# Four Strassen quads in each output projection of a two-layer decoder trunk, and six raw weight buffers

## The chip, the cores and the metric

The kernel runs on one core of a Trainium2 chip. Its time is the device time of one execution in microseconds, as the median of several; it was 2072.09 us over three runs (2071.94 to 2075.0). A core has five engines, each with its own queue of instructions: TensorE (PE in the profile: matmuls, with the weight loads as PEld), VectorE (DVE), ScalarE (ACT), GpSimd (POOL) and SyncE (SP), which here only issues transfers. Transfers run on 16 DMA engines.

## The reference

A decoder trunk of two layers over 256 tokens of width 2048, float32. Each layer is attention and then a gated feed-forward network with a causal convolution of width 3, each followed by a residual and a layer norm:

```python
for layer in range(DEPTH):                      # 2
    if layer < N_A_LAYERS:
        attn = moba_attention(h, moba_w_qkv[layer], moba_w_o[layer], rel_bias)
    else:
        attn = swa_attention(h, swa_w_q[j], swa_sinks[j], swa_w_o[j], k_band, v_band, ...)
    h = layer_norm(ALPHA * h + attn, ln_g[layer, 0], ln_b[layer, 0])
    ffn = conv_ffn(h, ffn_w_up[layer], ffn_conv_w[layer], ffn_conv_b[layer], ffn_w_down[layer])
    h = layer_norm(ALPHA * h + ffn, ln_g[layer, 1], ln_b[layer, 1])
```

The output projection at the end of an attention is `o @ w_o`, a 256 x 2048 by 2048 x 2048 product; the down-projection at the end of a feed-forward network is 256 x 5504 by 5504 x 2048.

## The kernel before, in words

**Precision.** Every float32 operand is split in a high and a low part (`float32r`), and a product is three matmuls: high by high, high by low, low by high (`product`, L503 to L511).

**Weights.** They come as a stream of halves: 128 x 1024 float32, 512 KB, which is two blocks of 128 x 512. `load_weights` (L135) loads a half into one of `RAW_BUFS` = 5 raw buffers from SP's queue. `high_upto` (L149) copies it to its high part on ScalarE (L159), `low_piece` (L166) subtracts on VectorE for the low part (L168). Both go to one of `HALF_BUFS` = 4 pairs of buffers, and TensorE reads them there. `split_upto(i)` splits up to half i and, after each, issues the load that takes the raw buffer that has become free. `take()` (L203), called before a half is used, splits up to three halves ahead (`AHEAD`). Where `reach` names a half, it splits further ahead, into memory that is idle by then (`aside`, `home`): the last eight halves of a projection (`WINDOW`) are run for token tile 0 first and then for token tile 1, so that all eight have to be there at once, and the layer norm of tile 0 runs beside tile 1's matmuls.

**Order.** The order is written out by hand. Work besides the matmuls is put on an agenda: `at(n, f)` queues f for VectorE, ScalarE and the queues n slots later, `pe_at` for TensorE. A slot is one half (`step`). Within `take()` the splits come first and then the slot's agenda; in a half that `reach` names, the agenda runs before the splits as well.

**Strassen quads.** In the down-projections, for two blocks of rows (a pair) and two chunks of 512 columns, the four weight blocks B11, B12, B21, B22 against two token tiles would be eight products. Seven are made, with sums of weights T1 to T4 and sums of activations. `presums` (L417) makes the weight sums during earlier stages: two loads of 512 KB on SP's queue, three subtractions or additions on VectorE (L427, L430, L431), and a store of 1 MB to DRAM on GpSimd's queue; the sums then come back as two halves of the stream, (T1, T3) and (T2, T4). `sums(i)` (L560) makes the activation sums of a group of two pairs in three steps on the agenda: `whole` adds high and low part (L566), `combine` makes the sums in a second work buffer (L575), `split` makes their high part on ScalarE (L579) and their low part on VectorE (L580), in memory of `xT`, which is idle then. A group of two pairs is seven halves (`SEVEN`); `PLAINS` says how many plain halves stand ahead of each group. `fold` (L536) adds the four products P1, P5, P6, P7 of two chunks to the result. A plain half has twelve matmuls, a half of a quad six.

**The output projections** (`project_out`, called at L826) have no quads before: 32 plain halves, chunk after chunk. The heads' outputs, which they read, are made by `attention`; the last heads' outputs come in the projection's first slots.

## Time and profile before

| | |
|---|---|
| Median of three runs | 2072.09 us |
| The profiled execution's own time | 2071.97 us |
| Its span, first to last instruction | 2070.2 us |
| TensorE busy | 2049.3 us (99%) |
| VectorE busy | 1656.4 us (80%) |
| ScalarE busy | 1039.4 us (50%) |
| DMA | 520.48 MB, 251 GB/s mean |
| Mean granted clock of TensorE | 0.998 |

The stages, by the busy time in each: layer 0's attention to 301 us, its output projection to 392, the opening of the feed-forward network to 444, the rest of its up-projection to 877, the down-projection to 1101; then layer 1 in the same order, with its output projection from 1260 to 1352 and its down-projection from 1837 on. A line of the timeline is: start, duration, engine, line, operation, out<-in, shapes, count, and in brackets how long the engine had stood idle before it and what ended that. Matmuls overlap, so a matmul's duration is longer than the distance to the next.

### The profile page before, as it was taken

The numbers are of one execution on the slowest core, as the hardware profiler recorded it, in microseconds if no ns is written. First come the engines' busy times: TensorE is split into PE (matmuls) and PEld (weight loads), VectorE is DVE, ScalarE is ACT, GpSimd is POOL, SyncE is SP. The second block draws the span as 40 slices with busy tenths as digits, with TensorE's granted clock in tenths as the row PEclk, the third lists the DMA queues.
The fourth block names the chain that finished last, engine by engine and source line by source line (L and its number), as shares of the span: only waits on it lengthen the run. The fifth ranks groups of instructions, "written<-read, shape, count | busy, mean of one in ns | idle before, by whom it ended". The sixth has DMA issues, their size and how long they took to land.

```text
span 2070.2 us, 29436 instructions
## 1 busy us (share of the span) xinstructions
PE 2049.3 (99%) x10956; PEld 1770.5 (86%) x10956; DVE 1656.4 (80%) x2388; ACT 1039.4 (50%) x1471; POOL 46.5 (2%) x76
## 2 busy tenths in 40 slices
PE   9999999999999999999999999999999999999997
PEld 7888888888888888888888888898888888888886
DVE  5666567689888888888786787679898888888877
ACT  4444445344444444465663455435444444456563
POOL 0100000000000000000000000000000000000000
PEclk9999999999999999999999999999999999999999
DMA  8757757368878778788884866737787877868894
GB/s 284 268 193 254 274 174 256 107 225 278 278 273 276 271 277 267 241 279 291 291 302 154 286 218 237 254 113 271 268 282 269 274 272 270 274 223 296 271 317 148
DMA packets 140190, 520.48 MB, mean 251 GB/s; under 512 B 18528, under 2 KB 18848, under 8 KB 133648
## 3 DMA queue, kind: packets, MB, share of 16 engines
q1 hardware_dynamic: 126992, 457.08, 65.4%
q0 software_dynamic: 12768, 61.27, 7.7%
q8 instruction: 86, 1.41, 0.3%
q14 instruction: 56, 0.46, 0.1%
q10 hardware_dynamic: 288, 0.26, 0.0%
HBM read 474.42 MB, written 48.28 MB: 252 GB/s over the span
## 4 chain that ended last, share of the span: by engine, by line
PE 93%; DVE 4%; DMA 1%; ACT 1%; issue 1%; SPq 0%; DVEq 0%; ACTq 0%
PE acc L313 37%; PE acc L315 19%; PE acc L509 7%; PE acc L510 7%; PE acc L511 7%; PE acc L376 2%; PE acc L377 2%; PE acc L378 2%; PE at L510 2%; PE at L511 2%; PE at L509 2%; PE acc L340 1%; DVE wl L168 1%; DMA raw<-in_wst_dram 1%; PE at L696 1%
## 5 line engine op out<-in xcount | busy, mean ns | idle before, releaser
L168 DVE TENSOR_TENSOR wl<-raw,wh 128x1024 fp32r<-128x1024 f32 (+1 forms) x723 | 863.1, 1220 | 158.2 <-ACT wh L159 142.3
L159 ACT ACTIVATE wh<-raw 128x1024 fp32r<-128x1024 f32 (+1 forms) x723 | 740.0, 1054 | 238.7 <-PE acc L511 92.8
L313 PE MATMUL acc<-xT,wh 128*128 128x512 f32 x3456 | 832.7, 392 | 0.0
L313 PEld LDWEIGHTS acc<-xT,wh 128*128 128x128 f32 x3456 | 641.2, 188 | 128.4
L315 PEld LDWEIGHTS acc<-xT,wl 128*128 128x128 f32 x3456 | 444.1, 190 | 17.1 <-DVE wl L168 4.4
L315 PE MATMUL acc<-xT,wl 128*128 128x256 f32 x3456 | 453.6, 284 | 3.1 <-DVE wl L168 3.1
L873 ACT ACTIVATE h<-acc 128x256 f32<-128x256 f32 x172 | 65.7, 382 | 319.2 <-PE acc L315 180.7
L874 DVE TENSOR_TENSOR h<-acc,h 128x256 f32<-128x256 f32 x172 | 72.5, 421 | 70.4 <-ACT h L873 70.4
L509 PE MATMUL acc<-wh,up 128*128 128x512 f32 x323 | 125.7, 389 | 0.0
L510 PE MATMUL acc<-wl,up 128*128 128x512 f32 x323 | 125.7, 389 | 0.0
L511 PE MATMUL acc<-wh,up 128*128 128x512 f32 x323 | 125.6, 389 | 0.0
L876 DVE SCALAR_TENSOR_TENSOR c<-h,cw,c 128x255 f32<-128x255 f32 x172 | 83.2, 484 | 6.1
L877 DVE SCALAR_TENSOR_TENSOR c<-h,cw,c 128x254 f32<-128x254 f32 x172 | 83.2, 483 | 6.2
L875 DVE TENSOR_SCALAR c<-h,cw 128x256 f32<-128x256 f32 x172 | 71.1, 413 | 6.2
L509 PE MATMUL acc<-wh,st 128*128 128x512 f32 x184 | 72.9, 396 | 0.0
L511 PE MATMUL acc<-wh,st 128*128 128x512 f32 x184 | 71.7, 390 | 0.0
L510 PE MATMUL acc<-wl,st 128*128 128x512 f32 x184 | 71.7, 390 | 0.0
L511 PEld LDWEIGHTS acc<-wh,up 128*128 128x128 f32 x323 | 60.6, 188 | 12.6
L509 PEld LDWEIGHTS acc<-wh,up 128*128 128x128 f32 x323 | 60.6, 188 | 12.6
L510 PEld LDWEIGHTS acc<-wl,up 128*128 128x128 f32 x323 | 60.6, 188 | 12.4
L376 PE MATMUL acc<-wh,xT 128*128 128x512 f32 x144 | 59.0, 410 | 1.3 <-ACT wh L159 1.3
L804 ACT ACTIVATE qT<-acc 128x256 f32<-128x256 f32 x32 | 12.3, 384 | 90.8 <-PE acc L315 66.3
(177 smaller groups left out, 2138.2 us busy)
## 6 DMA issues: line engine op xcount, KB each, us to landing
raw<-in_wst_dram SPq DMA_DIRECT2D x703, 512.0 KB, 4.6
gb<-in_wsum_dram SPq DMA_DIRECT2D x80, 512.0 KB, 7.2
ws<-gb POOLq DMA_DIRECT2D x40, 1024.0 KB, 5.4
raw<-ws SPq DMA_DIRECT2D x80, 512.0 KB, 5.5
band<-ud POOLq DMA_DIRECT2D x8, 512.0 KB, 14.9
bias<-band POOLq DMA_DIRECT2D x8, 512.0 KB, 6.4
gb<-in_ln_g_dram POOLq DMA_DIRECT2D x4, 1024.0 KB, 8.1
gb<-in_ln_b_dram POOLq DMA_DIRECT2D x4, 1024.0 KB, 11.3
```

What stands on the lines that cost most here:

```text
L159: nc.scalar.activation(wh[:, c], raws[s][:, c], AF.Copy)
L168: nc.vector.tensor_tensor(out=wl[:, c], in0=raws[s][:, c], in1=wh[:, c].bitcast(F32), op=ALU.subtract)
L313: nc.tensor.matmul(acc, w, xT[:, k, :], start=(k == 0), stop=(k == ends[0]))
L315: nc.tensor.matmul(acc[:, 0:T], w, xT[:, k, 0:T], start=False, stop=(k == ends[1]))
L376: nc.tensor.matmul(acc, sh, wh, start=(k == 0), stop=False)
L509: nc.tensor.matmul(acc, sh, wh, start=first, stop=False)
L510: nc.tensor.matmul(acc, sh, wl, start=False, stop=False)
L511: nc.tensor.matmul(acc, sl, wh, start=False, stop=last)
L874: nc.vector.tensor_tensor(out=h, in0=acc[:, 0:T], in1=h, op=ALU.add)
L875: nc.vector.tensor_scalar(c, h, w[:, 2:3], w[:, 3:4], op0=ALU.mult, op1=ALU.add)
L876: nc.vector.scalar_tensor_tensor(c[:, 1:T], h[:, 0:T - 1], w[:, 1:2], c[:, 1:T], op0=ALU.mult, op1=ALU.add)
L877: nc.vector.scalar_tensor_tensor(c[:, 2:T], h[:, 0:T - 2], w[:, 0:1], c[:, 2:T], op0=ALU.mult, op1=ALU.add)
```

## The change

- Each output projection now has four quads, in its first two chunks of columns, from the last eight of its sixteen row blocks. Its order (`PLAN_O`): 5 plain halves, 7 halves of quads, 1 plain, 7 of quads, 2 plain, and then 16 plain halves for the other two chunks. That is 38 halves in place of 32.
- The activation sums of the output projections have four members (s1, s3, s4, s2), since nothing is subtracted ahead of them; the down-projections keep three. All are made in place in one work buffer (`tmpp` has one buffer in place of two), and the layout in `xT` changes. The first group's steps are queued from slot 0 in the output projections (slot 1 in the down-projections), the second group's from slot 12.
- There are eight more quads whose weight sums are made ahead: eight quads in layer 0's attention (four before), four in layer 1's attention (four before, of other stages), 18 in each feed-forward network (16 before). In attention they are queued every six slots, not every nine. The VectorE steps come four and five slots after the first load, not five and six.
- `RAW_BUFS` is 6, in the memory of the second work buffer.
- The memory into which the output projections split ahead is ordered anew, and the ring is ten places long, not fourteen.

```diff
-RAW_BUFS = 5
+RAW_BUFS = 6
...
-EARLY = 4
+NQ_O = 4
+PLAINS_O = (5, 1, 2)
...
+def _mixed(c, groups, plain, p0):
+
+    plan, at = [], 0
+    for i, g in enumerate(groups):
+        plan += plain[at:at + g]
+        at += g
+        if i < len(groups) - 1:
+            plan += [tuple((b, p0 + 2 * i + p, c) for b, p in zip(bs, ps)) for bs, ps in zip(SEVEN, PAIR_OF)]
+    assert at == len(plain)
     return plan
...
+PLAN_O = _mixed(0, PLAINS_O, _plain(range(NH - 2 * NQ_O), (0, 1)), NH // 2 - NQ_O) + _plain(range(NH), (2, 3))
...
+QUADS = {}
+for _l in range(2):
+    QUADS[2 * _l] = [(2 * _l, 0, NH // 2 - NQ_O + p) for p in range(NQ_O)]
+    QUADS[2 * _l + 1] = [(2 * _l + 1, c, p) for c in range(2) for p in range(NQ)]
+ORDER = [q for li in range(4) for q in QUADS[li]]
+AHEAD_OF = {0: QUADS[0] + QUADS[1][:4], 1: QUADS[1][4:] + QUADS[3][:2], 2: QUADS[2], 3: QUADS[3][2:]}
...
-    tmpp = ctx.enter_context(tc.tile_pool(name="tmpp", bufs=2))
+    tmpp = ctx.enter_context(tc.tile_pool(name="tmpp", bufs=1))
...
-            at(m + 5, first)
-            at(m + 6, second, q)
+            at(m + 4, first)
+            at(m + 5, second, q)
...
-            g, s = [], []
+            g = []
 
             def whole():
                 g.append(tmpp.tile([P, HW], F32, name="tmp"))
...
             def combine():
...
+                a11, a21, a12, a22 = (g[0].rearrange("p (q s c) -> p s q c", q=2, s=4)[:, j] for j in range(4))
+                if ns == 3:
+                    ops = (a22, a22, a21, ALU.subtract), (a21, a22, a11, ALU.add), (a12, a12, a22, ALU.subtract)
+                else:
+                    ops = ((a21, a11, a21, ALU.subtract), (a22, a22, a21, ALU.subtract), (a11, a22, a11, ALU.add),
+                           (a12, a12, a22, ALU.subtract))
+                for o, a, b, op in ops:
                     nc.vector.tensor_tensor(out=o, in0=a, in1=b, op=op)
 
             def split():
...
+                s = g[0].rearrange("p (q s c) -> p q s c", q=2, s=4)[:, :, 4 - ns:4, :]
+                hi, lo = (xsum(i, ns)[:, h] for h in range(2))
+                nc.scalar.activation(hi, s, AF.Copy)
+                nc.vector.tensor_tensor(out=lo, in0=s, in1=hi.bitcast(F32), op=ALU.subtract)
...
         if quads:
-            for i in range(NQ // 2):
-                m = sum(PLAINS[0][:i]) + 7 * i if i else 1
+            groups = PLAINS[0] if ns == 3 else PLAINS_O
+            for i in range(len(groups) - 1):
+                m = sum(groups[:i]) + 7 * i if i else ns == 3
                 for j, f in enumerate(sums(i)):
                     at(m + j, f)
...
-        presums([(l, *q) for q in QUAD_ORDER[:EARLY]], 4 if l else 40, 9)
+        presums(AHEAD_OF[2 * l], 4 if l else 36, 6)
...
-        return project_out(lambda k: oT[:, k, :], PLAN_O, 2 * l, turnover.homes, AF.Gelu_apprx_tanh, turnover)
+        return project_out(lambda k: oT[:, k, :], PLAN_O, 2 * l, turnover.homes, AF.Gelu_apprx_tanh, turnover,
+                           lambda i: oT[:, NH - 2 * NQ_O + 4 * i:NH - 2 * NQ_O + 4 * i + 4, :])
...
-            return x + h[:4] + HALF_BUFS * [None] + h[4:], x + h[:4], h[4:] + h[:2]
+            places = [x[0], x[2], x[3], h[0], x[1], h[1], h[2], h[3]]
+            return places[:6] + HALF_BUFS * [None], places, h[4:] + h[:2]
...
-            presums([(l, *q) for q in QUAD_ORDER[EARLY:]], 0, 9)
+            presums(AHEAD_OF[2 * l + 1], 0, 9)
```

More of the change, by code (lines that the diff above doesn't have):

```diff
@@ L107, in trunk @@
     gbp = ctx.enter_context(tc.tile_pool(name="gbp", bufs=1))
-    tmpp = ctx.enter_context(tc.tile_pool(name="tmpp", bufs=2))
-    wsums = {(l, c, p): dram.tile([P, 2 * HW], F32, name=f"ws{l}{c}{p}")
-             for l in range(2) for c in range(2) for p in range(NQ)}
+    tmpp = ctx.enter_context(tc.tile_pool(name="tmpp", bufs=1))
+    wsums = {q: dram.tile([P, 2 * HW], F32, name="ws" + "_".join(map(str, q))) for q in ORDER}
     source, taken = [], 0
-    for stage_halves, l in _stages():
+    for stage_halves, li in _stages():
         for half in stage_halves:
@@ L116, in trunk @@
                 j = 0 if half[0][0] == "T1" else 1
-                source.append((wsums[l, half[0][2], half[0][1]], j))
+                source.append((wsums[li, half[0][2], half[0][1]], j))
             else:
@@ L437, in presums @@
             at(m + 1, load, q, 1)
-            at(m + 5, first)
-            at(m + 6, second, q)
+            at(m + 4, first)
+            at(m + 5, second, q)
     def project_out(src, plan, li, homes, preload, turnover=None, quad_blocks=None):
         mv = Moving(src, 0)
-        quads = any(_summed(half) for half in plan)
+        quads = bool(quad_blocks)
+        p0, ns = (NH // 2 - NQ_O, 4) if li % 2 == 0 else (0, 3)
         w0 = nexth["i"] + len(plan) - WINDOW
@@ L475, in project_out @@
         for i in range(2):
-            if quads:
+            if ns == 3:
                 at((whole - 4, len(plan) - WINDOW - 5)[i], load_gb, i)
@@ L490, in target @@
                 return [((n, t), *token(src(k), t)) for t in range(2)]
-            k1, k2, far = src(2 * k), src(2 * k + 1), xsum(k // 2)
+            k1, k2, far = src(2 * k), src(2 * k + 1), xsum((k - p0) // 2, ns)
             n0, n1 = 2 * n, 2 * n + 1
-            s1, s2, s4 = (tuple(far[:, h, j, k % 2, :] for h in range(2)) for j in range(3))
+            far = [tuple(far[:, h, k % 2, j, :] for h in range(2)) for j in range(ns)]
+            s1, s3, s4, s2 = (far[0], token(k1, 1), *far[1:]) if ns == 3 else far
             return [{"B11": (("P1", n), *token(k1, 0)), "B21": ((n0, 0), *token(k2, 0)), "T1": (("P5", n), *s1),
-                     "T3": (("P7", n), *token(k1, 1)), "T2": (("P6", n), *s2), "T4": ((n0, 1), *token(k2, 1)),
+                     "T3": (("P7", n), *s3), "T2": (("P6", n), *s2), "T4": ((n0, 1), *token(k2, 1)),
                      "B22": ((n1, 0), *s4)}[b]]
@@ L517, in zs @@
             return res[:, t, n * 512:(n + 1) * 512]
-        parts = {(t, n): 1 + (2 if (t, n % 2) == (1, 1) else 1) * quads for t in range(2) for n in range(NCH)}
+        paired = {e[2] for half in plan for e in half if e[0] == "B11"}
+        parts = {(t, n): 1 + (2 if (t, n % 2) == (1, 1) else 1) * (n // 2 in paired) for t in range(2) for n in range(NCH)}
         scaled = set()
@@ L675, in project_out @@
             for c in range(2):
-                if quads and c not in folded and done(*[(b, c) for b in SUMS]):
+                if c in paired and c not in folded and done(*[(b, c) for b in SUMS]):
                     folded.add(c)
@@ L971, in _planned, with _quads @@
     return np.stack([np.concatenate([block(*e) for e in half], 1) for half in plan if not _summed(half)])
-def _quads(w):
-    plan = [[(b, p, c) for b in ("B11", "B12", "B22", "B21")] for c in range(2) for p in range(NQ)]
-    return _planned(w, plan).reshape(2, NQ, P, 2 * HW)
+def _quads(ws):
+    return np.stack([_planned(ws[li], [[(b, p, c) for b in ("B11", "B12", "B22", "B21")]])[0] for li, c, p in ORDER])
 def _stream(w_qkv, w_o0, w_kv, w_q, w_o1, w_up, w_down):
@@ L1014 @@
                        a["ffn_w_up"], a["ffn_w_down"]),
-        "wsum": np.stack([_quads(a["ffn_w_down"][l]) for l in range(2)]),
+        "wsum": _quads([a["moba_w_o"][0], a["ffn_w_down"][0], a["swa_w_o"][0], a["ffn_w_down"][1]]),
         "xT": x.reshape(T, KB, P).transpose(2, 1, 0),
```

50 lines of the change are left out of this document (15 added, 35 removed).

## The prediction

> **What bounds the kernel now.** I read the first page from the top, then TensorE's waits, then single stretches of the timeline.
>
> ```profile
> span 2070.2 us, 29436 instructions
> PE 93%; DVE 4%; DMA 1%; ACT 1%; issue 1%; SPq 0%; DVEq 0%; ACTq 0%
> ...
> PE acc L315 <- DVE wl L168: 3.1, 4, 0.9
> PE at L607 <- DVE res L598: 1.6, 1, 1.6
> ...
> PE at L510 <- DVE wl L168: 1.0, 2, 0.5
> ```
>
> The chain that ended last is TensorE for 93%, and TensorE's waits are a few us in all. A matmul less is time won, and a new wait of TensorE is time lost, one for one. Every 0.2% is 4.1 us (about what a measurement of this kernel can tell from no change), so waits of a few us decide.
>
> The pace, and the room of the other engines inside a quad, show in the down-projection of layer 0, which already has quads (columns: start, duration, engine, line):
>
> ```profile
> 889.38 0.39 PE L509 MATMUL at<-wh,xT 128*128 128x512 f32 x1
> ...
> 890.74 0.39 PE L509 MATMUL at<-wh,xT 128*128 128x512 f32 x1
> ...
> 888.27 1.06 ACT L159 ACTIVATE wh<-raw 128x1024 fp32r<-128x1024 f32 x1 [0.93 <-ACT xT L579]
> 889.63 1.06 ACT L159 ACTIVATE wh<-raw 128x1024 fp32r<-128x1024 f32 x1 [0.30 <-PE acc L511]
> ...
> 889.37 3.94 DVE L168 TENSOR_TENSOR wl<-raw,wh 128x1024 fp32r<-128x1024 f32 x3 [0.63 <-ACT wh L159]
> ```
>
> Two halves of a quad start 1.36 us apart with six matmuls between: 0.227 us each (the 0.39 us overlap). A plain half has twelve: 2.72 us. ScalarE's copy of the half three places ahead starts 0.25 us after TensorE starts a half (889.63 against 889.38): with four buffers it has to wait until TensorE leaves one. VectorE's low part follows 1.10 us after that (889.37 against 888.27) and takes some 1.2 us. So quads are fed just in time, and VectorE can't run ahead.
>
> **The change, part by part.**
>
> *Matmuls.* A quad has seven products for eight, three matmuls each. Four quads in two stages remove 4 x 3 x 2 = 24 matmuls: 24 x 0.227 = **-5.4 us**.
>
> *The sums of activations, second group.* This is the term that decides. An output projection now runs five plain halves (places 0 to 4), seven of quads (5 to 11), one plain (12), seven of quads (13 to 19), and plain ones to place 37. The first group's sums are queued in slots 0, 1 and 2, before their use at place 6: covered by plain halves. The second group's are queued in slots 12, 13 and 14, and place 14 is the half T1/T3, whose very first matmul reads them. The down-projection has three plain halves at that point, this stage one. What these steps cost:
>
> ```profile
> 900.53 1.22 DVE L566 TENSOR_TENSOR tmp<-st 128x1024 f32<-128x1024 f32 x1
> 901.76 1.23 DVE L168 TENSOR_TENSOR wl<-raw,wh 128x1024 fp32r<-128x1024 f32 x1
> 902.90 1.21 DVE L575 TENSOR_TENSOR tmp<-tmp 128x256 f32<-128x256 f32 x3
> 904.28 1.23 DVE L168 TENSOR_TENSOR wl<-raw,wh 128x1024 fp32r<-128x1024 f32 x1 [0.16 <-ACT wh L159]
> 905.42 0.95 DVE L580 TENSOR_TENSOR xT<-tmp,xT 128x768 fp32r<-128x768 f32 x1
> ...
> 904.15 0.85 ACT L579 ACTIVATE xT<-tmp 128x768 fp32r<-128x768 f32 x1
> ...
> 907.06 0.39 PE L509 MATMUL at<-wh,xT 128*128 128x512 f32 x1
> ```
>
> In the down-projection the low part of the sums ends at 906.37 and T1 starts at 907.06: 0.69 us to spare. Now the same in the output projection, counted from TensorE's start of place 12. It starts place 13 at 2.72 and would start place 14 at 4.08. Within a slot the split of the half three places ahead comes first, then the step.
>
> - Slot 12: low part of half 15 on VectorE 1.35 to 2.57; whole sum (1.22) to 3.7.
> - Slot 13: half 16 can't start before TensorE has left half 12: ScalarE from 2.97, VectorE 4.07 to 5.29; then four combining operations for three, 1.21 + 0.45 = 1.67, to 6.9.
> - Slot 14: low part of half 17, queued ahead of the sums', to 8.0; meanwhile ScalarE copies the high part of the sums, now 1024 columns (1.06), 6.9 to 8.0; VectorE makes their low part, 8.0 to 9.2.
>
> T1's third matmul needs that low part and would have stood at 4.08 + 2 x 0.227 = 4.5. TensorE stands for 9.2 - 4.5 = 4.7 us, twice: **+9.4 us** (4.2 to 5.2 each: less if neighbouring operations overlap by 0.1 as these rows do, more if a load lands late). Behind the waiting matmul all of TensorE is queued, so nothing wins it back.
>
> *The clock after such a stop.* The stretches of the start and of the one longer stop later (columns after the stretch: its length, busy time of TensorE, weight loads, VectorE, ScalarE, GpSimd, granted clock, DMA share, GB/s):
>
> ```profile
> 8.69:12.10 3.41, 1.57 (x6) 1.08 (x7) 2.24 (x3) 3.05 (x4) 0.00 (x0) 1.00 1.03 413
> 12.10:15.51 3.41, 3.41 (x10) 2.63 (x9) 3.24 (x4) 2.26 (x4) 0.00 (x0) 0.50 1.04 352
> 15.51:18.92 3.41, 3.41 (x16) 2.79 (x15) 2.49 (x3) 2.55 (x4) 0.00 (x0) 1.00 0.99 336
> ...
> 1090.77:1094.18 3.41, 2.26 (x10) 1.53 (x9) 2.94 (x7) 0.29 (x1) 0.00 (x0) 1.00 0.97 330
> ```
>
> A stretch with TensorE busy 1.57 of 3.41 us was followed by one at half clock; one with 2.26 was not. The new stop is idle some 3.7 us, then two matmuls, then 0.8 us more: a 3.41 us stretch inside it is far below half busy. One stretch at half clock costs 3.41/2 = 1.7 us, less where it lies in the stop, up to twice that if the stop spoils two stretches. I take 1.5, twice: **+3.0 us** (0 to 6.8).
>
> [...]
>
> *Six raw buffers.* They pay where a chain of loads holds TensorE. There is one such place, the last halves of layer 0's down-projection:
>
> ```profile
> 1087.05 1.06 ACT L159 ACTIVATE up<-raw 128x1024 fp32r<-128x1024 f32 x1 [0.59 <-DMA raw<-in_wst_dram]
> 1088.67 1.06 ACT L159 ACTIVATE up<-raw 128x1024 fp32r<-128x1024 f32 x1 [0.56 <-DMA raw<-in_wst_dram]
> ...
> 1089.77 1.22 DVE L168 TENSOR_TENSOR up<-raw,up 128x1024 fp32r<-128x1024 f32 x1 [0.40 <-ACT up L159]
> 1090.91 0.68 DVE L525 TENSOR_TENSOR res<-res,acc 128x512 f32<-128x512 f32 x1
> ...
> 1094.66 0.55 PE L607 MATMUL at<-ident,res 128*128 128x128 f32 x3 [1.63 <-DVE res L598]
> ```
>
> ScalarE waits for loads, VectorE for ScalarE, the normalisation starts late, and TensorE's transposes wait 1.63 us. A load issued one split earlier takes most of that: **-1.5 us** (-1.7 to 0). At the kernel's start one more pair of loads now stands ahead of the bias tables on SP's queue: 768 KB at 336 GB/s, 2.3 us. The mask table was issued at 9.30 and lands 6.1 us later; TensorE uses it at 20.83, so 3 us are left: 0.
>
> ```profile
> 9.30 0.31 SPq L274 DMA_DIRECT2D us<-in_umask_dram  x1
> ...
> us<-in_umask_dram SPq DMA_DIRECT2D x1, 48.0 KB, 6.1
> ...
> 20.83 0.81 PE L279 MATMUL at<-oh,rb 32*16 32x384 f32 x2
> ```
>
> *More work for VectorE, later in the stage.* Six more splits (6.8), the second sums (4.1) and a fold (eight operations of 0.68, 5.4) fall between place 12 and the end of the first token tile: 16 us.
>
> ```profile
> 320.00:380.00 60.00, 60.00 (x267) 49.69 (x266) 42.20 (x41) 31.71 (x31) 0.00 (x0) 1.00 0.75 263
> ...
> L545 DVE TENSOR_TENSOR tmp<-at,tmp x4: 674/684/692, 975.4 to 2023.5; 128x512 f32<-128x512 f32 x4
> ...
> 380.17 0.69 DVE L527 SCALAR_TENSOR_TENSOR res<-res,acc 128x512 f32<-128x512 f32 x1 [6.57 <-PE acc L511]
> ...
> 383.12 0.75 DVE L598 SCALAR_TENSOR_TENSOR res<-res,rs,gb 128x512 f32<-128x512 f32 x1
> ...
> 385.42 0.60 PE L607 MATMUL at<-ident,res 128*128 128x128 f32 x4
> ```
>
> VectorE has 17.8 us free in those 60, 6.57 of them just ahead of the normalisation, and the transposes have another 1.5 (383.87 to 385.42). The stop adds time for it. I take 0; if only half of that free time lay where it can be used, 16 - 17.8/2 - 1.5, some 5.5 us a stage, would be the bound.
>
> *Weight sums.* Eight more quads of sums: two loads, three VectorE operations (2.6 us) and a store each, spread over attention and feed-forward; the VectorE steps come one slot sooner after the loads, at a pitch of six slots for nine in attention.
>
> ```profile
> L427 DVE TENSOR_TENSOR gb<-gb x40: 1214/1218/1226, 145.9 to 1769.4; 128x1024 f32<-128x1024 f32 x40
> ...
>   DVE gb L427: 0.5, 1
> ...
> DMA to landing us min/median/max: 4.1/6.3/12.5
> 444.00:877.00 433.00, 433.00 (x2484) 381.92 (x2483) 383.77 (x598) 209.21 (x311) 10.94 (x18) 1.00 0.78 269
> 1128.00:1262.00 134.00, 134.00 (x786) 118.67 (x785) 101.99 (x215) 72.19 (x162) 7.81 (x11) 1.00 0.70 237
> ```
>
> VectorE waited for these loads 0.5 us in all. A slot less (2484 matmuls in 433 us, 16 to a slot: 2.8 us) makes some wait, with the next weights' splits queued behind. VectorE has 49 us free in a feed-forward stage and 32 in layer 1's attention; I take 0, with 0 to +2.
>
> *One work buffer.* It is held from the whole sum to the split, 900.53 to 906.37, under 6 us, and groups are seven slots (9.5 us) or more apart: 0. The other form of the sums has the same column counts in the down-projections: 0.
>
> **Sum.** The profiled execution took 1.8 us more than its span, 2071.97, 0.1 below the median of the runs shown, 2072.09. 2071.97 - 5.4 + 9.4 + 3.0 - 1.5 = **2077.5 us**, +0.27%.
>
> **The rivals.**
> - *The stop, but no half clock:* 2071.97 - 5.4 + 9.4 - 1.5 = 2074.5, no change that can be told. For it: the stretch with 2.26 us of work, a third of it idle, left the clock alone. Against it: the one with 1.57. [...]
> - *No stop:* VectorE reaches the second sums in time, because splits run further ahead than I count, and only the matmuls and the loads tell: 2071.97 - 5.4 - 1.5 = 2065.1. For it: the down-projection's sums make their date. Against it: that had three plain halves of cover, and the 0.25 us rows tie the splits to TensorE.
> - *A late window besides:* VectorE's 16 us aren't hidden before the transposes; 2 us a stage on top of the forecast: 2081.5. For it: the fold falls among splits that have to run ahead. Against it: the 6.57 us.
>
> **Chances.** Forecast 0.45 (its own range 2075.5 to 2080), stop without half clock 0.25, no stop 0.13, late window 0.10, something not seen 0.07. Slower than 2076.2: most of the first (0.39), a little of the second (0.05), the late window (0.10), 0.02 of the rest: 0.56. Within 0.2%: 0.06 + 0.20 + 0.03 = 0.29. Faster: 0.13 + 0.02 = 0.15. The range 2070 to 2082 leaves out the case without a stop and the far ends.
>
> **What would show it.** Right: in both output projections one wait of TensorE on the sums' line of some 4.7 us, at the second T1, with VectorE and ScalarE without a pause ahead of it, and a 3.4 us stretch at half clock behind it; 24 matmuls fewer; the 1.63 us at L607 gone. Wrong: no wait there (the stop is a misreading of the order), a wait there below 3 us, or new waits at the transposes, which would be the window's.

## The result, and the profile after

The changed kernel takes 2084.62 us (median of four executions, 2083.99 to 2085.53), against 2072.10 us for the kernel before on the same chip: a ratio of 1.0057 [1.004, 1.0075]. It is slower, as forecast, but by 12.5 us where 5.5 were forecast, and outside the range.

The line numbers of the changed kernel are a little higher: the matmuls of a product are L513 to L515 (L509 to L511 before), of the up-projection and attention L315 and L317 (L313 and L315), a split is L160 on ScalarE and L169 on VectorE, the steps of the weight sums are L429, L432 and L433, the sums of activations L571, L582, L587 and L588, and the transposes L615. The first page, after, with the shares of the chain of waits:

```profile
span 2082.2 us, 29577 instructions
...
PE 88%; DVE 7%; DMA 2%; ACT 1%; issue 1%; SPq 0%; DVEq 0%; ACTq 0%
```

TensorE's waits, after (engine and line, what it waited for, us in total, times, longest):

```profile
PE at L513 <- ACT xT L587: 7.5, 2, 3.7
PE acc L317 <- DVE wl L169: 4.6, 8, 0.8
PE at L704 <- DVE qT L814: 1.8, 1, 1.8
...
PE at L731 <- DVE L L726: 1.2, 1, 1.2
...
PE at L615 <- DVE res L606: 0.2, 1, 0.2
```

TensorE's share of the chain of waits has gone from 93% to 88%, and VectorE's from 4% to 7%. The first row is the stop that was forecast, once in each output projection. The transposes' wait of 1.6 us is down to 0.2. The waits at L704 and L731, both in layer 1's attention, and the longer one at L317 are new. The prediction says that some steps of the weight sums would wait, "with the next weights' splits queued behind", but it prices these waits at nothing.

A stage is taken here from the start of its first matmul to that of the next stage's. "Start" is all before the first unit of layer 0's attention; a feed-forward stage includes its opening. Stage lengths against the kernel before, in us, from one profiled execution of each kernel:

| kernel | start | att. 0 | out 0 | ffn 0 | down 0 | att. 1 | out 1 | ffn 1 | down 1 |
|---|---|---|---|---|---|---|---|---|---|
| after | -1.9 | 0.0 | **+4.3** | +1.9 | -1.9 | **+4.6** | **+4.2** | +0.7 | 0.0 |
| early | -0.3 | 0.0 | -0.2 | +1.0 | -1.9 | +4.9 | -1.6 | +0.7 | 0.0 |
| busy | -2.0 | 0.0 | +2.1 | +0.7 | -1.9 | +6.6 | +2.1 | +1.1 | -0.1 |
| slots | -1.9 | 0.0 | +4.1 | 0.0 | -0.3 | 0.0 | +3.5 | -0.1 | +0.1 |
| raw5 | -1.9 | +0.1 | +4.6 | +1.3 | +1.7 | +7.1 | +5.4 | +0.9 | +1.9 |
| early_slots | -2.1 | -0.1 | -1.2 | 0.0 | -0.3 | 0.0 | -2.0 | -0.1 | -0.1 |
| es_pool2 | -2.0 | -0.1 | +3.2 | +0.2 | -1.8 | 0.0 | -0.3 | -0.1 | -0.1 |
| before6 | -0.3 | -0.1 | 0.0 | 0.0 | -1.9 | 0.0 | 0.0 | 0.0 | -0.1 |
| es_raw5 | -2.0 | -0.1 | +3.1 | +0.4 | +2.5 | 0.0 | +2.3 | -0.1 | 0.0 |
| es_nq2 | -0.4 | 0.0 | -0.7 | 0.0 | -0.1 | 0.0 | -0.7 | -0.1 | -0.1 |
| pitch9 | -2.1 | 0.0 | +4.4 | +0.9 | -1.9 | +0.6 | +3.7 | +1.0 | 0.0 |
| es_six0 | -2.0 | -0.1 | -0.8 | 0.0 | -1.9 | 0.0 | -1.1 | -0.1 | -0.1 |
| es_nq2_moved | -1.6 | -0.1 | -1.4 | 0.0 | -1.9 | 0.0 | -1.4 | -0.1 | -0.1 |

The first row adds up to +11.9 us, the difference of the two spans being 12.0. Three places carry it: the two output projections, the second attention, and the first feed-forward stage. The start is no part of the change: it is 0.3 us or 1.6 to 2.1 us shorter in one execution or another, whatever was edited. There is a stretch at half clock in it before (0.50 from 12.10 to 15.51), in `early` and in `before6` (each 0.3 us shorter than before); in the changed kernel, `busy`, `slots`, `early_slots`, `es_pool2` and `es_raw5` (1.9 to 2.1 us shorter) the granted clock was 1.00 throughout the first 20 us.

The stop in the first output projection, after (timeline: start, duration, engine, line, operation; TensorE, then VectorE, then ScalarE):

```profile
328.86 0.39 PE L515 MATMUL acc<-wh,st 128*128 128x512 f32 x1
332.98 0.80 PE L513 MATMUL at<-wh,xT 128*128 128x512 f32 x1 [3.73 <-ACT xT L587]
333.57 0.63 PE L514 MATMUL at<-wl,xT 128*128 128x512 f32 x1
334.24 0.80 PE L515 MATMUL at<-wh,xT 128*128 128x512 f32 x1
...
330.62 1.22 DVE L582 TENSOR_TENSOR tmp<-tmp 128x256 f32<-128x256 f32 x3
331.75 1.22 DVE L169 TENSOR_TENSOR wl<-raw,wh 128x1024 fp32r<-128x1024 f32 x1
332.96 1.23 DVE L588 TENSOR_TENSOR xT<-tmp,xT 128x1024 fp32r<-128x1024 f32 x1
...
331.87 1.06 ACT L587 ACTIVATE xT<-tmp 128x1024 fp32r<-128x1024 f32 x1 [1.53 <-DVE tmp L582]
```

TensorE starts place 12 at 324.97. The high part of the sums starts 6.9 us later (331.87) and the low part ends 9.22 us later (334.19), to the tenth the 6.9 and 9.2 of the prediction's timetable; the third matmul of T1 starts at 334.24. The clock around it, after (columns as in the prediction: the busy times of TensorE and the others, and third from the end the granted clock):

```profile
327.90:331.33 3.43, 1.35 (x6) 0.77 (x5) 3.00 (x5) 2.12 (x2) 0.00 (x0) 1.00 1.02 419
331.33:334.74 3.41, 1.72 (x3) 1.00 (x4) 2.86 (x4) 1.06 (x1) 0.00 (x0) 0.50 0.75 261
334.74:338.16 3.42, 3.42 (x9) 2.64 (x9) 0.67 (x1) 1.06 (x1) 0.00 (x0) 0.50 0.26 98
338.16:341.57 3.41, 3.41 (x16) 2.80 (x15) 2.34 (x3) 2.87 (x4) 0.00 (x0) 1.00 0.44 154
```

Two stretches run at half clock (0.50), not one. The second has 9 matmuls where the next has 16.

The second attention, after (VectorE's timeline, and the issue of the load that it waits for, on SP):

```profile
1154.41 1.23 DVE L429 TENSOR_TENSOR gb<-gb 128x1024 f32<-128x1024 f32 x1 [2.98 <-DMA gb<-in_wsum_dram]
...
1169.44 0.42 DVE L814 TENSOR_TENSOR qT<-acc,qT 128x256 f32<-128x256 f32 x1
1175.25 1.23 DVE L429 TENSOR_TENSOR gb<-gb 128x1024 f32<-128x1024 f32 x1 [5.39 <-DMA gb<-in_wsum_dram]
1176.39 0.15 DVE L722 TENSOR_TENSOR sm<-sm,es 128x2 f32<-128x2 f32 x1
1176.58 0.17 DVE L724 RECIPROCAL rsm<-sm 128x2 f32<-128x2 f32 x1
1176.78 0.55 DVE L726 TENSOR_SCALAR L<-L,rsm 128x128 f32<-128x128 f32 x2
1177.24 2.35 DVE L169 TENSOR_TENSOR wl<-raw,wh 128x1024 fp32r<-128x1024 f32 x2
...
1162.24 2.03 SPq L426 DMA_DIRECT2D gb<-in_wsum_dram  x1
```

From the view of the tile `gb` in the same stage, how long its loads took:

```profile
DMA to landing us min/median/max: 5.3/8.4/12.9
```

VectorE stands for 5.39 us until the load issued at 1162.24 has landed, the 12.9 us of the second row. That load is the second of its sum: the two are issued a slot apart (the first at 1158.53), and the step needs both. Queued behind the waiting step are the softmax's division (L724, L726), for which the transposes at L731 wait, and the splits of the next weights (L169). TensorE's three waits in this stage (1.2 us at L731, 0.5 at L317, 1.8 at L704) all come in the 8 us behind this step.

In the feed-forward stages the landing times are ordinary, and the steps wait all the same. One sum of the first feed-forward stage, after and then before (the issue of its second load, then the step):

```profile
629.68 0.42 SPq L426 DMA_DIRECT2D gb<-in_wsum_dram  x1
636.71 1.23 DVE L429 TENSOR_TENSOR gb<-gb 128x1024 f32<-128x1024 f32 x1 [2.29 <-DMA gb<-in_wsum_dram]
```

```profile
626.25 1.26 SPq L424 DMA_DIRECT2D gb<-in_wsum_dram  x1
636.93 1.22 DVE L427 TENSOR_TENSOR gb<-gb 128x1024 f32<-128x1024 f32 x1
```

After, VectorE is ready for the step 4.7 us behind the issue (636.71 less 2.29, less 629.68), and the load takes 6.9 us. Before, the step comes 10.7 us behind the issue, and the load, which took 5.9 us, has long landed. VectorE's idle time ahead of these steps in that stage is 7.5 us after and 0.0 before.

### The profile page after: what moved, and what is told of

Same layout as the page of the kernel before. It is cut to its first block, busy times and chain, and to the rows that moved or that the text cites. A ratio compares the mean times of both kernels' runs of the same rounds, so it can differ in the third digit from the quotient of the medians.

```text
span 2082.2 us, 29577 instructions
## 1 busy us (share of the span) xinstructions
PE 2051.5 (99%) x10932; PEld 1769.9 (85%) x10932; DVE 1710.8 (82%) x2464; ACT 1055.1 (51%) x1489; POOL 51.1 (2%) x84
## 4 chain that ended last, share of the span: by engine, by line
PE 88%; DVE 7%; DMA 2%; ACT 1%; issue 1%; SPq 0%; DVEq 0%; ACTq 0%
PE acc L315 34%; PE acc L317 18%; PE acc L513 7%; PE acc L515 7%; PE acc L514 7%; DVE wl L169 3%; PE at L515 2%; PE at L514 2%; PE at L513 2%; PE acc L379 2%; PE acc L378 2%; PE acc L380 2%; PE acc L342 1%; DMA gb<-in_wsum_dram 1%; ACT wh L160 1%
## 5 line engine op out<-in xcount | busy, mean ns | idle before, releaser
L169 DVE TENSOR_TENSOR wl<-raw,wh 128x1024 fp32r<-128x1024 f32 (+1 forms) x741 | 883.6, 1220 | 144.3 <-ACT wh L160 122.2
L160 ACT ACTIVATE wh<-raw 128x1024 fp32r<-128x1024 f32 (+1 forms) x741 | 758.4, 1054 | 241.3 <-PE acc L515 131.2
L315 PE MATMUL acc<-xT,wh 128*128 128x512 f32 x3456 | 832.4, 392 | 0.0
L315 PEld LDWEIGHTS acc<-xT,wh 128*128 128x128 f32 x3456 | 641.9, 188 | 127.5
L317 PEld LDWEIGHTS acc<-xT,wl 128*128 128x128 f32 x3456 | 444.2, 190 | 20.3 <-DVE wl L169 7.2
L317 PE MATMUL acc<-xT,wl 128*128 128x256 f32 x3456 | 455.3, 285 | 4.6 <-DVE wl L169 4.6
L513 PE MATMUL acc<-wh,up 128*128 128x512 f32 x323 | 125.8, 390 | 0.0
L515 PE MATMUL acc<-wh,up 128*128 128x512 f32 x323 | 125.8, 390 | 0.0
L429 DVE TENSOR_TENSOR gb<-gb 128x1024 f32<-128x1024 f32 x48 | 58.6, 1221 | 22.0 <-DMA gb<-in_wsum_dram 18.1
L515 PEld LDWEIGHTS acc<-wh,up 128*128 128x128 f32 x323 | 60.7, 188 | 12.5
L513 PEld LDWEIGHTS acc<-wh,up 128*128 128x128 f32 x323 | 60.7, 188 | 12.5
L514 PEld LDWEIGHTS acc<-wl,up 128*128 128x128 f32 x323 | 60.7, 188 | 12.5
L196 ACT ACTIVATE c<-c 128x256 f32<-128x256 f32 x86 | 36.0, 419 | 56.4 <-DVE c L888 52.2
L513 PE MATMUL acc<-wh,st 128*128 128x512 f32 x160 | 63.9, 399 | 0.0
L514 PE MATMUL acc<-wl,st 128*128 128x512 f32 x160 | 62.8, 393 | 0.0
L515 PE MATMUL acc<-wh,st 128*128 128x512 f32 x160 | 62.6, 391 | 0.0
## 6 DMA issues: line engine op xcount, KB each, us to landing
gb<-in_ln_b_dram POOLq DMA_DIRECT2D x4, 1024.0 KB, 10.7
```

The source lines that it names most:

```text
L160: nc.scalar.activation(wh[:, c], raws[s][:, c], AF.Copy)
L169: nc.vector.tensor_tensor(out=wl[:, c], in0=raws[s][:, c], in1=wh[:, c].bitcast(F32), op=ALU.subtract)
L315: nc.tensor.matmul(acc, w, xT[:, k, :], start=(k == 0), stop=(k == ends[0]))
L317: nc.tensor.matmul(acc[:, 0:T], w, xT[:, k, 0:T], start=False, stop=(k == ends[1]))
L513: nc.tensor.matmul(acc, sh, wh, start=first, stop=False)
L514: nc.tensor.matmul(acc, sh, wl, start=False, stop=False)
```

## The experiments

Times are medians, ratios are to the kernel before in the same session. Its median was 2070.79 us beside `early`, `busy`, `slots` and `raw5`; 2071.62 beside `early_slots`, `es_pool2`, `before6` and `es_raw5`; 2070.53 beside `es_nq2` and `pitch9`; 2070.40 beside `es_six0` and `es_nq2_moved`.

### early: the second sums four places sooner

```diff
-                m = sum(groups[:i]) + 7 * i if i else ns == 3
+                m = (sum(groups[:i]) + 7 * i if ns == 3 else 8) if i else ns == 3
```

> The second group's activation sums are queued in slots 8, 9 and 10 of an output projection, not 12, 13 and 14. Theory 1: the stop of TensorE at the second T1 (3.7 us idle, then the half clock behind it) is the whole loss of these two stages, which took 4.3 and 4.2 us more than before; without it each takes 2.7 us less than before (24 matmuls) but for some 0.2 us: 2084.6 - 2 x 6.8 = 2071. Theory 2: VectorE is full there anyway (7 us idle between 322 and 382 us in the changed kernel, all of it around the stop); the wait moves to the transposes of the window, up to 5 us a stage: 2075 to 2081.

2074.15 us, a ratio of 1.0012 [1.0002, 1.0022]. Neither output projection has a wait at the sums, nor a stretch at half clock (the granted clock is 1.00 in every row there). But they are 0.2 and 1.6 us shorter than before, not the 2.7 us of the twelve matmuls. TensorE's wait that is new there, 1.6 us in the first and 0.6 in the second (the rest of what is missing, 0.9 and 0.5 us, stands in no wait of the view):

```profile
PE at L615 <- DVE res L606: 2.2, 2, 1.6
```

VectorE's timeline ahead of it in the first output projection:

```profile
377.68 1.22 DVE L169 TENSOR_TENSOR wl<-raw,wh 128x1024 fp32r<-128x1024 f32 x1
378.82 2.35 DVE L169 TENSOR_TENSOR up<-raw,up 128x1024 fp32r<-128x1024 f32 x2
381.09 0.68 DVE L532 SCALAR_TENSOR_TENSOR res<-res,acc 128x512 f32<-128x512 f32 x1
```

Before, VectorE stood idle for 6.57 us ahead of that evacuation. Now it comes to it straight from the splits, and the transposes wait. The prediction's cover for VectorE's 16 us was there in the changed kernel only because the stop gave VectorE the time.

### busy: the stop without the idle TensorE

```diff
+            if ns == 4 and i == 14:
+                for _ in range(16):
+                    nc.tensor.matmul(banks["P1", 0], token(src(8), 0)[0], blocks[0][0], start=False, stop=False)
```

> Sixteen more matmuls stand ahead of the second T1 in each output projection; they fill 3.6 of the 3.7 us in which TensorE stood idle (their result is added to one product's bank, so the output is not the reference's). Theory 1: the half clock (6.83 us at 0.50 in both stages) comes from the idle time alone, and costs 3.4 us a stage: with TensorE busy the stop is as long as it was, the clock stays, 2084.6 - 6.8 = 2077.8. Theory 2: the cost behind the stop is late operands, not the clock: nothing is won, 2084.6.

2080.78 us, 1.0049 [1.0034, 1.0064]. With sixteen added matmuls in the stop the granted clock stays at 1.00 in both output projections, and they are 2.1 us longer than before, not 4.3 and 4.2. The 2.1 us are about the stop (4.7) less the matmuls saved (2.7). So, by the difference of the two runs, the half clock behind the stop cost 2.0 to 2.2 us in each. The second attention is 6.6 us longer here, not 4.6: a stretch at half clock (0.50) follows the waits there at 1176.00, which the changed kernel doesn't have (`early` has one too, at 1175.44, and 4.9 us).

### slots and pitch9: what makes the second attention longer

`slots` puts the VectorE steps of the weight sums back, `pitch9` the distance between sums in the second attention:

```diff
-            at(m + 4, first)
-            at(m + 5, second, q)
+            at(m + 5, first)
+            at(m + 6, second, q)
```

> The VectorE steps of the weight sums come five and six slots after the first load again, as before the change; all else is as changed. Theory 1: the slot that was taken away makes VectorE wait for the loads; layer 1's attention (+4.6 us) and the feed-forward stages (+1.9 and +0.7) go back to before: 2084.6 - 7.2 = 2077.4. Theory 2: in layer 1's attention the pitch of six slots does it, since a load there took 12.9 us to land; only the feed-forward stages win: 2082.

```diff
-        presums(AHEAD_OF[2 * l], 4 if l else 36, 6)
+        presums(AHEAD_OF[2 * l], 4 if l else 36, 9 if l else 6)
```

> The change with the weight sums of the second attention nine slots apart instead of six, their VectorE steps four and five slots behind the loads as in the change. Theory 1 (the step comes too soon for a load that takes 8 to 13 us, and each too early step costs what is missing; the distance between sums has nothing to do with it): the second attention is 2 to 5 us longer than before, as in the change. Theory 2 (six slots apart, with the earlier steps, a load queues up behind the store of the sum before, and that makes it late): the second attention within 0.5 us of before. In both, all other stages are as in the change (+4.3 and +4.2 in the output projections).

`slots`: 2077.48 us, 1.0033 [1.0019, 1.0046]. The second attention and both feed-forward stages are back to the length before, with as many sums as in the changed kernel and six slots apart. `pitch9`: 2078.91 us, 1.0038 [1.0024, 1.0052]; the second attention is 0.6 us longer than before, the feed-forward stages 0.9 and 1.0 us, as they are not touched. VectorE's work on the sums in that stage (columns of groups: shapes, count, busy and mean, then idle time before them and what ended it), `slots` and then `pitch9`:

```profile
L429 DVE TENSOR_TENSOR gb<-gb 128x1024 f32<-128x1024 f32 x4 | 4.9, 1220 | 0.3 <-DMA gb<-in_wsum_dram 0.3
```

```profile
L429 DVE TENSOR_TENSOR gb<-gb 128x1024 f32<-128x1024 f32 x4 | 4.9, 1216 | 3.5 <-DMA gb<-in_wsum_dram 3.5
```

In the changed kernel the same group is idle for 8.4 us before it. The early step alone (`pitch9`) lets VectorE wait 3.5 us and costs TensorE 0.6; the shorter distance alone (`slots`) costs nothing; both together cost 4.6. `pitch9` came out as neither theory had it: the first theory's mechanism acts, but at this distance it costs little. That loads land later when sums are closer is not shown: the longest landing is 12.9 us in the changed kernel, 11.4 in `pitch9`, and 11.1 in `slots`, which has the shorter distance too. The traces show another difference. In `pitch9` the second load of the second sum is issued 12.3 us ahead of its step (1168.31 and 1180.58), and nothing waits; in the changed kernel VectorE is ready for that step 7.6 us behind the issue (1175.25 less 5.39, less 1162.24). No run separates this from the landing time.

### before6, raw5 and es_raw5: the sixth buffer

`before6` is the kernel before with `RAW_BUFS = 6` and the sums made in place in one work buffer; `raw5` is the changed kernel with `RAW_BUFS = 5`.

> The kernel before with six raw buffers, and the one work buffer that makes room for them; no quads in the output projections, loads and steps of the weight sums as they were. Theory 1 (the sixth buffer alone takes the transposes' wait of 1.63 us at the end of the first down-projection): that stage is 1.7 to 1.9 us shorter, the rest within 0.3, the total 1.5 to 2.2 us below before, a ratio of 0.9989 to 0.9993. Theory 2 (the wait went because the weight sums of the feed-forward are made earlier, and with them at five and six slots it gives back most, as the run with the late steps hinted with its 0.34): that stage within 0.5 of before and the ratio 0.9997 to 1.0002. If the half-clock stretch of the start (12.10 to 15.51 before) is gone too, 1.7 us more are gained and this belongs to where that stretch falls, not to the buffers.

> Five raw buffers in place of six; all else is as changed. Theory 1: the sixth is worth what two stages won, 1.85 us in layer 0's down-projection and 1.9 us at the kernel's start: 2084.6 + 3.7 = 2088.3. Theory 2: the start is won by where the half-clock stretch of the start falls, not by the buffer: only the down-projection loses, 2086.5.

`before6`: 2068.67 us, 0.9989 [0.998, 0.9998]. One stage has changed, the first down-projection, by 1.85 us. Alone, this part of the change makes the kernel faster. `raw5`: 2089.9 us, 1.0097 [1.0082, 1.0113], 19.1 us above the kernel before in its session, where the changed kernel was 12.5 above. Its first down-projection loses the gain and 1.7 us more, and its output projections, second attention and second down-projection are longer too. Its start is as short as the changed kernel's, so that gain isn't the buffers'.

`es_raw5` is `early_slots` (below) with five:

> As early_slots, with five raw buffers. Theory 1 (the sixth buffer is worth its 1.5 to 1.9 us at the end of the first down-projection): that stage 1.5 to 2 us longer than in early_slots, the others within 0.5; ratio to early_slots 1.0007 to 1.001. Theory 2 (five buffers cost more in the output projections, where quads use up weights unevenly, as the run with five buffers hinted with +4.6 and +5.4 there against +4.3 and +4.2): the output projections are 1 us or more longer each besides, 4 us in all.

2078.58 us, 1.0038 [1.0025, 1.005]: 10.7 us above `early_slots`. Each output projection is 4.3 us longer than there, the first down-projection 2.9. Both theories acted, the second with more than its 1 us a stage. A buffer that is worth 1.85 us without quads in the output projections is worth nearly six times that with them: TensorE's waits for the transposes come to 6.2 us, and half clock follows two of them (0.50 from 384.8 to 388.2 and from 1350.7 to 1354.1).

### early_slots: both edits undone where they cost

```diff
-            at(m + 4, first)
-            at(m + 5, second, q)
+            at(m + 5, first)
+            at(m + 6, second, q)
...
-                m = sum(groups[:i]) + 7 * i if i else ns == 3
+                m = (sum(groups[:i]) + 7 * i if ns == 3 else 8) if i else ns == 3
```

> The change with the second sums at places 8 to 10 and the VectorE steps of the weight sums five and six slots behind their loads again. Theory 1 (the losses are separate and each edit takes its own away): stage by stage the one run's figure where its edit acts, -0.2 in the first output projection, -1.6 in the second, 0 in the second attention and in both feed-forwards, -0.3 to -1.9 at the end of the first down-projection, -0.3 to -1.9 at the start; 2.4 to 5.6 us below the kernel before, a ratio of 0.9973 to 0.9988. Theory 2 (the late steps of the weight sums come due where the new sums need VectorE, so that what the one edit gains the other gives back): the second output projection or the first down-projection loses 2 us or more against theory 1, and the ratio lies at 0.999 to 1.001.

2067.87 us, 0.9981 [0.9972, 0.999]: faster than before. The pieces add up: the attention and the feed-forward stages cost nothing, and the output projections gain 1.2 and 2.0 us. Two things are short of the whole. The transposes still wait 1.2 us in all, and the first down-projection gains 0.34 us where `before6` has 1.85. The two next experiments are about these.

### es_pool2: two steps of the sums on GpSimd

```diff
-                nc.vector.tensor_tensor(out=g[0].rearrange("p (a b) -> p a b", a=4), in0=x[:, :, 0:T].bitcast(F32),
-                                        in1=x[:, :, T:2 * T].bitcast(F32), op=ALU.add)
+                add = nc.vector if ns == 3 else nc.gpsimd
+                add.tensor_tensor(out=g[0].rearrange("p (a b) -> p a b", a=4), in0=x[:, :, 0:T].bitcast(F32),
+                                  in1=x[:, :, T:2 * T].bitcast(F32), op=ALU.add)
...
-                nc.vector.tensor_tensor(out=lo, in0=s, in1=hi.bitcast(F32), op=ALU.subtract)
+                (nc.vector if ns == 3 else nc.gpsimd).tensor_tensor(out=lo, in0=s, in1=hi.bitcast(F32), op=ALU.subtract)
```

> As early_slots, with the first and the last VectorE step of each sum (the sum of the high and low part, 1.216 us, and the low part of the result, 1.223 us; four steps and 4.9 us in an output projection) on GpSimd. Theory 1 (VectorE is what is late at the end of the output projections in the run with early sums, where TensorE waited 1.6 and 0.6 us for a row of the residual): both waits go and each output projection is 1.8 to 2.7 us shorter than before; 2.4 us in all below early_slots. Theory 2 (GpSimd takes several times as long as VectorE for such a step, or slows VectorE while it runs): TensorE stops at the first pair (place 5 or 6) or the second, and the run is 2 to 10 us above early_slots.

2069.53 us, 0.9996 [0.9987, 1.0004]: slower than `early_slots`. GpSimd's steps in the views of the tiles `tmp` and `xT` (count, then min, median and max in ns):

```profile
L572 POOL TENSOR_TENSOR tmp<-st x4: 2393/2402/2440, 271.1 to 1279.2; 128x1024 f32<-128x1024 f32 x4
L589 POOL TENSOR_TENSOR xT<-tmp,xT x4: 2403/2427/2552, 309.3 to 1288.9; 128x1024 fp32r<-128x1024 f32 x4
```

TensorE's wait at the transposes:

```profile
PE at L616 <- DVE res L607: 2.2, 2, 1.9
```

A step takes twice as long there (2.40 and 2.43 us, against 1.22 on VectorE). And VectorE got no relief: a split that starts while such a step runs takes 2.6 to 3.4 us in place of 1.22 (all seven that do). One of them, beside the step that GpSimd starts at 317.69, and TensorE's wait at a quad of the same stage:

```profile
317.69 2.40 POOL L572 TENSOR_TENSOR tmp<-st 128x1024 f32<-128x1024 f32 x1 [5.88 <-DVE st L745]
317.98 3.19 DVE L169 TENSOR_TENSOR wl<-raw,wh 128x1024 fp32r<-128x1024 f32 x1 [0.44 <-ACT wh L160]
330.94 0.50 PE L514 MATMUL at<-wl,xT 128*128 128x512 f32 x1 [1.26 <-DVE wl L169]
```

The wait at the quad is for a split that ran beside GpSimd's step of 327.40 to 329.81 and ended 2.59 us after its start. So the second theory is what happened (the run is 1.7 us above `early_slots`), and the first one, VectorE's lateness at the end, isn't tested by this run. Half clock (0.50 from 386.1 to 389.5) follows the wait at the end of the first output projection, which makes that stage 3.2 us longer.

### es_six0: fewer weight sums in the first feed-forward stage

In all runs with 18 sums in that stage, the copy of the second attention's bias stands behind their stores in GpSimd's queue. It is issued 1 to 8 us ahead of the down-projection, not 50. The issue in the view of the tile `band`, in the kernel before, in `early_slots` and in `es_six0` (duration in ns, then the start in us):

```profile
L288 POOL DMA_DIRECT2D band<-ud x1: 1132/1132/1132, 825.4 to 825.4; - x1
```

```profile
L290 POOL DMA_DIRECT2D band<-ud x1: 1142/1142/1142, 872.2 to 872.2; - x1
```

```profile
L290 POOL DMA_DIRECT2D band<-ud x1: 1139/1139/1139, 821.8 to 821.8; - x1
```

The waits of `early_slots` at the opening of the first down-projection:

```profile
ACT wh L160 <- DMA raw<-ws: 3.2, 2, 1.7
...
PE at L514 <- DVE wl L169: 0.8, 1, 0.8
```

```diff
-AHEAD_OF = {0: QUADS[0] + QUADS[1][:4], 1: QUADS[1][4:] + QUADS[3][:2], 2: QUADS[2], 3: QUADS[3][2:]}
+AHEAD_OF = {0: QUADS[0] + QUADS[1][:6], 1: QUADS[1][6:] + QUADS[3][:2], 2: QUADS[2], 3: QUADS[3][2:]}
...
-        presums(AHEAD_OF[2 * l], 4 if l else 36, 6)
+        presums(AHEAD_OF[2 * l], 4 if l else 30, 6)
```

> As early_slots, with two weight sums of the first down-projection made in the first attention instead of the first feed-forward (ten there, from slot 30, six slots apart; sixteen in the first feed-forward, as many as before the change). In every run of the change the copy of the second attention's bias, band<-ud on GpSimd's queue, is issued at 870 to 877 us, behind the last stores of the weight sums, where the kernel before issued it at 825; it takes 17 to 20 us to land. Theory 1 (this copy runs into the loads at the opening of the first down-projection, and in early_slots, where it is issued 1.5 us before that stage, two loads of weight sums come 1.5 us late for it): it is issued near 825 again, the wait of TensorE at 893 to 896 us goes, the first down-projection is 1.85 us shorter than before instead of 0.34, the rest as in early_slots; 1.5 us below early_slots, a ratio to before of 0.9970 to 0.9985. Theory 2 (those loads are late for another reason, such as the step of the last weight sum): that stage stays at 0 to -0.4 and the time at that of early_slots.

2066.18 us, 0.9979 [0.9971, 0.9988]. The first down-projection is 1.87 us shorter than before and TensorE has no wait at its opening: as the first theory had it, for that stage. But with sixteen sums in the stage the loads and the steps of the last sums are gone from that date too, so the run doesn't tell the copy from them. The total gained less than the 1.5 us, since the output projections, in which nothing was edited, took 0.4 and 0.9 us more than in `early_slots`; the ratios of the two can't be told apart. The changed kernel issued the copy 7.9 us ahead of the stage (873.5) and didn't lose there; `early_slots`, `slots` and `es_nq2`, 1.2 to 2.0 us ahead of it, did; `es_pool2`, 2.3 us ahead (876.1), didn't. So a copy just ahead of the stage fits the loss, and is not shown to be its cause.

### es_nq2 and es_nq2_moved: half as many quads

```diff
-NQ_O = 4
-PLAINS_O = (5, 1, 2)
+NQ_O = 2
+PLAINS_O = (10, 2)
...
-                m = (sum(groups[:i]) + 7 * i if ns == 3 else 8) if i else ns == 3
+                m = (sum(groups[:i]) + 7 * i if ns == 3 else 8) if i else (1 if ns == 3 else 6)
```

> As early_slots, with two quads instead of four in each output projection (the second pair alone, heads 12 to 15; its sums at places 6 to 8, its pair at places 10 to 16). 12 matmuls of 0.227 us less instead of 24 in the two stages together count 1.36 us a stage; the added work of VectorE (sums, splits of the added weights, folding) is half or a little more. Theory 1 (the output projections of early_slots end late by VectorE's backlog, 1.1 and 0.2 us of waits at the transposes): with less added work no wait is left and both output projections are 1.3 to 1.4 us shorter than before; with the sixth buffer's 1.85, 4.5 us below before in all, a ratio of 0.9975 to 0.9985. Theory 2 (the waits come from the end of the plan alone, the splits for the window and the evacuations there, and not from what went before): the waits stay, each output projection gains 0.3 us or nothing, 2 us below before.

2069.34 us, 0.9989 [0.998, 0.9998]. No wait is left at the transposes, but each output projection gains 0.7 us only. This plan reads the sums until place 16, when weights for the stage's end are already split into their memory: TensorE waits for such a split there, and the last pairs multiply weights in place of sums. `es_nq2_moved` puts the sums elsewhere, and two weight sums into the second attention:

```diff
-AHEAD_OF = {0: QUADS[0] + QUADS[1][:4], 1: QUADS[1][4:] + QUADS[3][:2], 2: QUADS[2], 3: QUADS[3][2:]}
+AHEAD_OF = {0: QUADS[0] + QUADS[1][:4], 1: QUADS[1][4:], 2: QUADS[2] + QUADS[3][:2], 3: QUADS[3][2:]}
...
-            k1, k2, far = src(2 * k), src(2 * k + 1), xsum((k - p0) // 2, ns)
+            k1, k2, far = src(2 * k), src(2 * k + 1), xsum((k - p0) // 2 + (ns == 4), ns)
...
-                hi, lo = (xsum(i, ns)[:, h] for h in range(2))
+                hi, lo = (xsum(i + (ns == 4), ns)[:, h] for h in range(2))
```

> As es_nq2 (two quads in each output projection, heads 12 to 15), with the sums in the second half of the space that the change uses for them, where no weights of the stage's end are split to before the quads are through (in es_nq2 they were, so its last pairs multiply weights instead of sums), and two weight sums of the second down-projection made in the second attention instead of the first feed-forward. Theory 1 (the 0.7 us that es_nq2's output projections lacked against 1.36 each are the wait for that space, 0.77 and 0.34 between matmuls at 337 us, and nothing of VectorE's backlog): both output projections 1.3 to 1.4 us shorter than before; the bias copy is issued near 825 and the first down-projection 1.85 us shorter; 4.5 us below before, a ratio of 0.9972 to 0.9985. Theory 2 (the low parts there are late by VectorE's backlog at any place): a wait of 0.3 to 0.8 us at the quads stays and the output projections gain 0.7 or less.

2065.67 us, 0.9975 [0.9966, 0.9984], the lowest ratio of all, though it can't be told from that of `es_six0`. Both output projections gain 1.36 us, which is six matmuls of 0.227 us to the hundredth. All of TensorE's waits in it:

```profile
PE acc L317 <- DVE wl L169: 3.0, 4, 0.8
PE at L260 <- POOL ident masks.py:199: 1.4, 1, 1.4
PE at L514 <- DVE wl L169: 1.0, 2, 0.5
PE acc L378 <- ACT wh L160: 0.8, 1, 0.8
PE acc L379 <- DVE wl L169: 0.8, 1, 0.8
```

Four quads could save 2.7 us a stage, and no run got that: `early_slots` came nearest, with 1.2 and 2.0. They bring VectorE 19 us more work (82.8 of 93 us busy in the first output projection of `early`, 63.9 before). That this is why they fall short is likely, but argued: `es_pool2`, which was to take work off VectorE, didn't. Two quads save 1.36 and get all of it.

## Why the prediction was wrong, step by step

- **Matmuls, -5.4.** Right: `es_nq2_moved` gains exactly 0.227 us for each matmul less.
- **The stop, +9.4.** Right: 4.72 us (334.19, when the low part ended, less 329.47, which is the start of place 12 and the prediction's 4.5 us to T1's third matmul), and the same stop in the second output projection. `busy`, with the stop alone, has 4.7 - 2.7 = 2.0 us a stage forecast and 2.1 measured. The rival without a stop is out.
- **The clock, +3.0.** That half clock would follow the stop was right (0.50 from 331.33 to 338.16, behind 1.35 us of work in 3.43, and from 1300.70 to 1307.52, behind 0.89 in 3.41); the size was too small: 2.2 and 2.0 us, 4.2 in all. The half clock lasted 6.83 us, two stretches; the first lies mostly in the stop, the second doesn't. So the two output projections are 8.5 us longer, for 7.0 forecast. The rival without half clock is out.
- **Six raw buffers, -1.5.** Right: -1.85, shown alone by `before6`. That quads would make the sixth buffer worth 11 us, and that the change could hardly do without it, the prediction didn't see.
- **VectorE later in the stage, 0.** Right for this kernel (0.2 us at the transposes), for a reason that it names in half a sentence only: the stop adds time. Once the stop is gone the waits are 1.6 and 0.6 us, the "late window" rival in small. That this term came out at nothing was in part luck.
- **Weight sums, 0 (0 to +2).** This is the step that failed: +4.6 us in the second attention and +2.5 in the feed-forward stages, 7.1 in all. The prediction set VectorE's idle time in the stage (32 us) against the added work, as if it were a question of load. It is one of dates: `slots` has the same sums at the old dates and pays nothing. The prediction counts only the slot that goes ("one slot sooner after the loads"), not what is left. A step needs both loads, and the second leaves a slot later than the first, so the change left it three slots in place of four. In the first feed-forward stage VectorE was ready for the four steps whose idle time is put to a load 4.7 to 4.8 us behind the issue of the second load, and these loads took 5.4 to 6.9 us, about the median of 6.3 that the prediction quotes. Before, every such step of that stage came 9.0 us or more behind it, and no load took over 8.8. In layer 1's attention the two waiting steps had 7.9 and 7.6 us, for loads of 10.7 and 12.9. While one waited (5.39 us), the attention's softmax and the next splits stood behind it. The six-slot distance was costed with it at nothing; alone it does cost nothing, and `slots` and `pitch9` show that most of the attention's 4.6 us needs both.
- **One work buffer, 0.** Right: `before6` has it, and no stage of it is longer.
- **The start, 0.** It was 1.9 us shorter in the profile, but `early`, which has the same start, is only 0.3 us shorter there, and `raw5`, with five buffers, 1.9: it goes with the execution, not with the change.

From the forecast of +5.5 it is +1.5 for the clock (with some tenths of the stop), +7.1 for the weight sums, -0.35 for the buffers and -1.87 for the start: +11.9, the sum of the stages.

## What to carry to other kernels

A step that waits for a transfer, and holds what is queued behind it on its engine (for 5.39 us in the second attention here), is to be dated from the issue of the last transfer that it needs, against the landing times in the trace, the longest too, and then everything queued behind it is to be named; idle time of the engine in the same stage says nothing about it. A stop worked out place by place from the durations of single rows can be right to a tenth of a microsecond, so it is worth doing for every wait that a change adds, not just for the one that looks worst. And an edit that moves several dates at once hides its gain: here the buffer, half the quads and the old dates together make the kernel 0.25% faster, where the change made it 0.57% slower.

## What the runs showed of the hardware that was not expected

In these runs the granted clock went from 1.00 to 0.50 behind, among others, stretches of 3.41 to 3.43 us in which TensorE was busy for 1.29 us (`es_raw5`), 1.35 us (the changed kernel) and 1.57 us (the kernel before), and it stayed at 0.50 for 3.4 or 6.8 us. The stretches below are laid end to end with the changes of the clock in the same profile. Where the end of an output projection waited 2.12 us in `es_raw5`:

```profile
1347.31:1350.72 3.41, 1.29 (x8) 0.84 (x7) 2.94 (x7) 0.29 (x1) 0.00 (x0) 1.00 0.94 362
1350.72:1354.13 3.41, 3.41 (x12) 2.71 (x11) 3.34 (x5) 0.75 (x2) 0.00 (x0) 0.51 0.02 8
1354.13:1357.54 3.41, 3.41 (x21) 2.84 (x19) 2.07 (x4) 1.99 (x3) 0.00 (x0) 0.99 0.00 0
```

Where it waited 1.61 us in `early`, and behind the waits in the second attention of the changed kernel:

```profile
383.54:386.95 3.41, 2.11 (x13) 1.81 (x14) 3.31 (x6) 0.60 (x1) 0.00 (x0) 1.00 0.56 210
```

```profile
1181.25:1184.66 3.41, 1.63 (x10) 1.34 (x9) 2.32 (x10) 1.80 (x6) 0.52 (x1) 1.00 0.87 263
```

2.11 us of work (`early`) and 2.26 (the kernel before, 1090.77 to 1094.18) were not followed by half clock. In between no single figure divides the cases: 1.63 us (the changed kernel) was not followed by it, and 1.66 or more was (`before6`, 8.58 to 11.99, an estimate: its rows 6.82:10.23 and 10.23:13.64 have 2.17 and 2.90 us of work, and at most 3.41 of that lie outside the stretch). Waits of 1.61 us (`early`) and 1.63 us (the kernel before) were followed by no half clock; those of 1.94 us (`es_pool2`), 2.12 and 2.5 us (`es_raw5`) by 3.4 us of it. But in `raw5` waits of 2.1 us at the transposes of the first down-projection and of 2.3 us in the second attention brought none (0.95 in every row there); the stretch at the former (1096.32 to 1099.73) still had at least 1.70 us of work, since TensorE was busy throughout the row 1094.61:1098.02. So in these runs the length of a wait alone doesn't tell. Behind the stops of 3.7 us the half clock lasted 6.8 us, but 3.4 in the second output projection of `slots` (1297.6 to 1301.1). The stretch at half clock in `es_raw5` has 12 matmuls where the next has 21, so the wait of 2.12 us there cost nearly twice its length, by an estimate: 2.12 and half of 3.41 are 3.8. In the profiled execution of `raw5` the granted clock stood at 0.95 almost throughout (mean 0.944), and layer 0's attention, which has no new wait, was still as long as before, to 0.14 us.
